# Sums of squares for the main stream's norms: one matmul group per tile of squares in place of adding the tiles up first

## The chip, the cores and the metric

The kernel runs on one core of a Trainium2 chip. The metric is the time of one execution on the device in microseconds (us), the median of several runs. The engines of the core are the tensor engine (PE), the vector engine (DVE), the scalar engine (ACT), GpSimd (POOL) and SyncE (SP), which issues the transfers. Each has its own instruction stream, and they wait for each other through semaphores. [...]

## The reference

The model is two stacks of two layers at 512 tokens and width 1024. The first two layers are hybrids of attention, retention and gated linear attention; the other two have attention and a feed-forward part, and take a second stream of 256 context tokens along. All is float32. What the change touches are the norms of the main stream:

```python
def rms_norm(x, gain=None):
    xf = x.astype(jnp.float32)
    y = xf * lax.rsqrt(jnp.mean(xf * xf, axis=-1, keepdims=True) + EPS)
    ...

def second_block(...):
    ...
        h = rms_norm_2(x, norm_g[l, 0]) * (1.0 + sc1) + sh1
        ...
        x = x + g1 * rms_norm_2(y, norm_g[l, 1])
        h = rms_norm_2(x, norm_g[l, 2]) * (1.0 + sc2) + sh2
        x = x + g2 * rms_norm_2(swiglu(h, ffn_w_in[l], ffn_w_out[l]), norm_g[l, 3])
```

For each token the squares of its 1024 features are summed; the token's features are then scaled by the root's reciprocal, a gain and a shift.

## The kernel before, in words

Activations lie with the features on the 128 partitions and the tokens along the free dimension: `x` is eight tiles of 128 features by 512 tokens (`KD` = 8, `S` = 512; the context has `CL` = 256 tokens). A norm therefore needs a sum over partitions. It is made in these steps. `square` makes a tile's squares on ACT (line 503). `square_sums` adds the eight square tiles up on DVE: six adds at line 515 into the first two, one at line 518. `rstd_cols` then lets PE sum over the partitions: for each of four blocks of 128 tokens the 128x128 block of squares is the stationary operand and a column of ones (`blk`) the moving one, so that each matmul gives one column of 128 sums (the records `<-blk,bp 128x1` at line 389; a float32 matmul runs as two passes, so that four matmuls are eight records). DVE scales the sums (line 481), POOL takes the power -1/2 (line 483), and `spread` brings the result back to all partitions with four transposes (line 498, `<-ident,sm`). `norm_tile` then makes the pairs `hh`, `hl` of high and low parts (lines 554 to 560), from which the dense matmuls work: each product is three matmuls with high and low parts of weights and activations (`wh`, `wl`, made by ACT at line 422 and by POOL or DVE at lines 398 and 400 from the loaded `wr`).

Five times in the program `boundary` joins two layers' halves. It loads x, adds the normed output of the half before (`postnorm_tile`, lines 576 and 577; the adds into x are made by POOL and DVE in turns), stores x, makes the squares and sums, and norms x for the half behind. The square tiles come from the tag `bp`, which has five buffers, in the fifth boundary eight. Boundaries 1 to 4 (at about 464, 961, 1545 and 2030 us of the profile) are woven with work of the context stream, whose dense matmuls show as `<-hc,wh`, `<-hc,wl` and `<-hid,wh`; a function `weave` takes steps of the two streams by fixed rates, and a scheduler, which goes by planned times of the instructions, fixes the order on every engine. Boundary 5 (at 2444 us) is alone; behind it the first matmuls of the feed-forward part (`outer`) start on weights already held (`u0h` and so on).

Of the kernel before, what the change touches and what calls it, by code (L numbers as in the profile page):

```python
# [23 lines left out]
KD = D // 128  # L24
S = 512
# [174 lines left out]
class Net:  # L200
# [266 lines left out]
    def rstd_cols(self, sq_tiles, T, groups, width, add=False, al=None):  # L467

        nc = self.nc
        nt = T // 128  # L470
        groups, add = (self.ones_col, True) if groups is None else (groups, add)
        per = groups.shape[-1]
        n = per if add else per * len(sq_tiles)
        ps = (al or self.std)[1]([128, nt, n])
        m = len(sq_tiles)
        for i, sq in enumerate(sq_tiles):
            for t in range(nt):
                o = ps[:, t, :] if add else ps[:, t, i * per:(i + 1) * per]
                self.mm(o, sq[:, t * 128:t * 128 + 128], groups, i + t == 0, (i, t) == (m - 1, nt - 1))
        ms = self.sm([128, nt, n])  # L480
        nc.vector.tensor_scalar(ms, ps, 1.0 / width, EPS, op0=ALU.mult, op1=ALU.add)  # L481
        r = self.sm([128, nt, n])
        nc.gpsimd.tensor_tensor(r, ms, self.mhalf[:, None, :].to_broadcast([128, nt, n]), op=ALU.pow)  # L483
        return r
# [55 lines left out]
    def prenorm_steps(self, x, T, gain, shift, pool=None, al=None):  # L540

        nc = self.nc
        n = x.shape[1]
        r = self.rstd(self.square_sums([x[:, k, :] for k in range(n)], T, al), T, al=al)
        h = self.new_h(T, pool)
        for k in range(n):
            self.norm_tile(h, x, k, T, r, gain, shift, al)
            yield
        return h
# [1419 lines left out]
```

## Time and profile before

| | |
|---|---|
| median of 3 runs | 2850.54 us (2847.57 to 2851.17) |
| the profiled execution | 2850.94 us, span 2849.2 us |
| PE busy | 87% of the span |
| DVE, ACT, POOL busy | 44%, 42%, 38% |
| mean granted clock of PE | 0.913 |

The profile shows one execution. A busy share is a mean over all stages; which engine ends a wait in one stage is read from the timeline there, where the figure in brackets is the idle time before an instruction and what ended it.

### The profile page before, as it was taken

What the parts mean: (1) busy time and instruction counts of PE and PEld (TensorE: products, weight loads), DVE (VectorE), ACT (ScalarE), POOL (GpSimd) and SP (SyncE); (2) the same over time, 40 slices, a digit from 0 to 9 for tenths busy, and PEclk for the clock granted to TensorE, in tenths of its full rate; (3) what the DMA queues carried; (4) which work ended last, traced back from release to release, by engine and by line L of the source; (5) the groups of instructions that cost most, each with busy time, mean ns of one, the idle gap of its engine ahead of it and who ended that gap; (6) DMA issues with size and microseconds to landing.
All of it is one profiled execution on the core that took longest, in us unless ns stands there. A gap on an engine that the chain in (4) does not pass through costs nothing. (4 is left out here: it accounts for less than half of the span.)

```text
span 2849.2 us, 35397 instructions
## 1 busy us (share of the span) xinstructions
PE 2467.3 (87%) x13052; PEld 2004.1 (70%) x13052; DVE 1262.4 (44%) x2065; ACT 1187.1 (42%) x2227; POOL 1079.5 (38%) x754
## 2 busy tenths in 40 slices
PE   6978897778888886869999999999878969799997
PEld 4755676665666665648998877777766757688886
DVE  3655356245646643445443621212635757421212
ACT  3534364333547534445554422223434636333222
POOL 2435235344533541214355632323542222443334
PEclk9988897888989987879999999999988989899998
DMA  7354553344344652335554444453443254333332
GB/s 241 125 199 166 181 174 136 117 135 165 107 122 142 220 179 90 116 113 157 162 167 141 163 155 170 145 173 115 165 145 105 68 154 121 110 116 97 96 97 74
DMA packets 170817, 400.58 MB, mean 141 GB/s; under 512 B 19378, under 2 KB 60820, under 8 KB 167316
## 3 DMA queue, kind: packets, MB, share of 16 engines
q1 hardware_dynamic: 170644, 398.31, 42.9%
q8 instruction: 104, 1.70, 0.2%
q14 instruction: 69, 0.57, 0.1%
HBM read 339.85 MB, written 58.39 MB: 140 GB/s over the span
## 5 line engine op out<-in xcount | busy, mean ns | idle before, releaser
L398 POOL TENSOR_TENSOR wl<-wr,wh 128x1024 fp32r<-128x1024 f32 (+3 forms) x245 | 537.7, 2196 | 893.6 <-ACT wh L422 449.0
L422 ACT CAST wh<-wr 128x1024 fp32r<-128x1024 f32 (+3 forms) x367 | 353.8, 964 | 731.0 <-PE d L389 282.6
L389 PE MATMUL d<-hh,wh 128*128 128x512 f32 x960 | 399.1, 416 | 19.3 <-ACT hh L556 7.8
L389 PE MATMUL d<-hl,wh 128*128 128x512 f32 x960 | 394.9, 411 | 3.2 <-POOL hl L398 1.2
L389 PE MATMUL d<-hh,wl 128*128 128x512 f32 x960 | 262.0, 401 | 0.0
L400 DVE SCALAR_TENSOR_TENSOR wl<-wr,wh 128x1024 fp32r<-128x1024 f32 (+3 forms) x122 | 151.9, 1245 | 228.8 <-PE d L389 97.9
L389 PEld LDWEIGHTS d<-hh,wh 128*128 128x128 f32 x960 | 190.5, 198 | 62.3 <-ACT hh L556 8.4
L389 PEld LDWEIGHTS d<-hl,wh 128*128 128x128 f32 x960 | 190.3, 198 | 43.2 <-issue 2.5
L389 PEld LDWEIGHTS d<-hh,wl 128*128 128x128 f32 x960 | 183.8, 193 | 39.2 <-issue 1.5
L400 DVE SCALAR_TENSOR_TENSOR pg<-b,pg 128x512 fp32r<-128x512 f32 (+1 forms) x208 | 137.1, 665 | 69.6 <-ACT pg L404 68.2
L934 POOL TENSOR_TENSOR oy<-pg,pg 64x256 f32<-64x256 f32 (+1 forms) x72 | 57.8, 802 | 284.4 <-ACT pg L931 89.4
L389 PE MATMUL b<-hh,wh 128*128 128x512 f32 x416 | 164.5, 395 | 0.0
L389 PE MATMUL b<-hl,wh 128*128 128x512 f32 x416 | 163.5, 393 | 0.0
L404 ACT CAST pg<-b 128x512 fp32r<-128x512 f32 (+1 forms) x208 | 117.3, 571 | 90.9 <-PE b L909 85.4
L882 DVE TENSOR_REDUCE sm<-s 128x1 f32<-128x768 f32 (+3 forms) x144 | 120.8, 846 | 63.8 <-PE s L389 63.4
L389 PE MATMUL d<-hc,wh 128*128 128x256 f32 x656 | 107.4, 315 | 24.2 <-ACT wh L422 11.7
L950 DVE SCALAR_TENSOR_TENSOR rp<-rp,d 128x512 f32<-128x512 f32 (+1 forms) x77 | 46.7, 607 | 166.1 <-ACT rp L949 166.0
L389 PEld LDWEIGHTS d<-hc,wh 128*128 128x128 f32 x656 | 97.0, 216 | 28.8 <-ACT wh L422 12.9
L389 PE MATMUL d<-hid,wh 128*128 128x512 f32 (+1 forms) x528 | 115.5, 363 | 1.6 <-POOL hid L398 1.5
L1738 DVE SCALAR_TENSOR_TENSOR rp<-rp,b 128x512 f32<-128x512 f32 (+1 forms) x64 | 38.1, 596 | 175.5 <-PE b L389 175.0
L389 PE MATMUL b<-hid,wh 128*128 128x512 f32 (+1 forms) x528 | 110.9, 361 | 0.0
L389 PE MATMUL b<-hh,wl 128*128 128x512 f32 x416 | 104.0, 390 | 0.0
(412 smaller groups left out, 5165.5 us busy)
## 6 DMA issues: line engine op xcount, KB each, us to landing
wr<-in_ffn_w_in SPq DMA_DIRECT2D x132, 512.0 KB
mr<-in_ada_w SPq DMA_DIRECT2D x96, 512.0 KB
wr<-in_ffn_w_out SPq DMA_DIRECT2D x48, 512.0 KB
x<-x SPq DMA_DIRECT2D x20, 1024.0 KB
wr<-in_w_in SPq DMA_DIRECT2D x38, 512.0 KB
mr<-in_w_mod SPq DMA_DIRECT2D x32, 512.0 KB
wr<-in_ev_w_in SPq DMA_DIRECT2D x20, 512.0 KB
wr<-in_ffn_w_out SPq DMA_DIRECT2D x24, 384.0 KB
```

Source lines behind the costliest of these rows:

```text
L389: self.nc.tensor.matmul(out, lhsT, rhs, start=start, stop=stop)
L398: self.nc.gpsimd.tensor_sub(out, src, hi)
L400: self.nc.vector.scalar_tensor_tensor(out, src, scale, hi, op0=ALU.mult, op1=ALU.subtract)
L404: self.nc.scalar.copy(hi, src)
L422: nc.scalar.copy(hi[:, :n], raw[:, :n])
L882: nc.vector.reduce_max(c, s, axis=AX.X, negate=True)
L934: nc.gpsimd.tensor_tensor(d, sel(t), sel(rs), op=ALU.mult)
L950: nc.vector.scalar_tensor_tensor(t, t, 1.0, ps, op0=ALU.add, op1=ALU.mult)
L1738: nc.vector.scalar_tensor_tensor(g, g, 0.5, pu, op0=ALU.mult, op1=ALU.mult)
```

## The change

In `prenorm_steps`, for the main stream alone (512 tokens), the squares are no longer added up on DVE. A generator hands the eight square tiles to `rstd_cols` one by one, which makes four matmuls from each and lets PE accumulate all 32 in one PSUM tile. The tile in PSUM is now taken before the first square is made, and the buffer of a square comes free when PE has read it. The context's norms and the start keep the adds.

```diff
--- before.py
+++ after.py
@@ -470,9 +470,9 @@
         nt = T // 128
         groups, add = (self.ones_col, True) if groups is None else (groups, add)
         per = groups.shape[-1]
-        n = per if add else per * len(sq_tiles)
+        m = len(sq_tiles) if isinstance(sq_tiles, list) else KD
+        n = per if add else per * m
         ps = (al or self.std)[1]([128, nt, n])
-        m = len(sq_tiles)
         for i, sq in enumerate(sq_tiles):
             for t in range(nt):
                 o = ps[:, t, :] if add else ps[:, t, i * per:(i + 1) * per]
@@ -541,7 +541,8 @@
 
         nc = self.nc
         n = x.shape[1]
-        r = self.rstd(self.square_sums([x[:, k, :] for k in range(n)], T, al), T, al=al)
+        xs = [x[:, k, :] for k in range(n)]
+        r = self.rstd(self.square_sums(xs, T, al) if T < S else (self.square(t, T, al) for t in xs), T, al=al)
         h = self.new_h(T, pool)
         for k in range(n):
             self.norm_tile(h, x, k, T, r, gain, shift, al)
```

The scheduler orders the instructions anew. The names in the rows that follow are the program's tiles with running numbers, which differ between the two programs; `x4` is four matmuls in succession. First, PE in boundary 5. Before (`b_21041` takes the sums of squares, `b_21050` the transposes):

```order
L389 MATMUL b_20974<-blk,rp_20962 128x1 x4
L498 MATMUL b_20987<-ident,sm_20985 128x128 x4
L389 MATMUL b_21041<-blk,bp_21018 128x1 x4
L498 MATMUL b_21050<-ident,sm_21048 128x128 x4
L389 MATMUL d_21093<-hh_21055,u0h_20782 128x512
```

After (`b_21102` takes the sums, from eight tiles `bp`):

```order
L498 MATMUL b_21071<-ident,sm_21069 128x128 x4
L389 MATMUL b_21102<-blk,bp_21103 128x1 x4
L389 MATMUL b_21102<-blk,bp_21109 128x1 x4
L389 MATMUL b_21102<-blk,bp_21115 128x1 x4
L389 MATMUL b_21102<-blk,bp_21121 128x1 x4
L389 MATMUL b_21102<-blk,bp_21127 128x1 x4
L389 MATMUL b_21102<-blk,bp_21133 128x1 x4
L389 MATMUL b_21102<-blk,bp_21139 128x1 x4
L389 MATMUL b_21102<-blk,bp_21145 128x1 x4
L498 MATMUL b_21155<-ident,sm_21153 128x128 x4
L389 MATMUL d_21198<-hh_21160,u0h_20866 128x512
```

The four matmuls on the added-up tile have become eight groups of four, contiguous, ahead of the same transposes. In boundaries 2 and 4 the eight groups stand contiguous too. In boundary 2 two products of the modulation (`<-mr,mc`) and its selections (`<-mod_sel`), which stood behind the transposes, now stand between the groups and the transposes. In boundary 4 ten matmuls `d<-hc` stood ahead of the group and five behind it; now all sixteen stand behind the transposes. In boundary 3 two groups are contiguous and the others are single matmuls between the context's feed-forward matmuls.

Second, PE in boundary 1, where `d_4015` and `d_4066` are pieces of the context's dense work. Before:

```order
L389 MATMUL d_4015<-hc_3692,wh_4011 128x256 x16
L389 MATMUL d_4015<-hc_3692,wl_4012 128x256 x8
L389 MATMUL d_4066<-hc_3692,wh_4062 128x256 x5
L389 MATMUL s_4157<-blk,bp_4134 128x1 x4
L389 MATMUL d_4066<-hc_3692,wh_4062 128x256 x5
L498 MATMUL s_4166<-ident,sm_4164 128x128 x4
L389 MATMUL d_4066<-hc_3692,wh_4062 128x256 x6
```

After (`s_4134` takes the sums of squares):

```order
L389 MATMUL s_4134<-blk,bp_4135 128x1 x4
L389 MATMUL s_4134<-blk,bp_4141 128x1 x4
L389 MATMUL d_4015<-hc_3692,wh_4011 128x256 x2
L389 MATMUL s_4134<-blk,bp_4147 128x1 x4
L389 MATMUL d_4015<-hc_3692,wh_4011 128x256 x3
L389 MATMUL s_4134<-blk,bp_4153 128x1 x4
L389 MATMUL d_4015<-hc_3692,wh_4011 128x256 x2
L389 MATMUL s_4134<-blk,bp_4159 128x1 x4
L389 MATMUL d_4015<-hc_3692,wh_4011 128x256 x2
L389 MATMUL s_4134<-blk,bp_4165 128x1 x4
L389 MATMUL d_4015<-hc_3692,wh_4011 128x256 x2
L389 MATMUL s_4134<-blk,bp_4171 128x1 x4
```

The first piece, `d_4015`, stood whole ahead of the one group; now two groups stand ahead of it, and the other six within it. The transposes have moved from the second piece into the end of the first.

Third, ACT in the same place, with the norm's first instructions (`hh`, `bp`) and the weight casts `wh`. Before:

```order
L406 ACTIVATE rp_4007<-d_4015 128x256
L556 ACTIVATE hh_4171<-bp_4173,m_110 128x512
L406 ACTIVATE rp_4058<-d_4066 128x256
L560 ACTIVATE bp_4177<-bp_4177,m_110 128x512
L556 ACTIVATE hh_4171<-bp_4182,m_110 128x512
L404 CAST hh_4171<-bp_4177 128x512
L422 CAST wh_4097<-wr_4095 128x1024
L560 ACTIVATE bp_4230<-bp_4230,m_110 128x512
L422 CAST wh_4188<-wr_4186 128x1024
```

After:

```order
L406 ACTIVATE rp_4007<-d_4015 128x256
L557 ACTIVATE hh_4192<-bp_4194,m_110 128x512
L561 ACTIVATE bp_4198<-bp_4198,m_110 128x512
L404 CAST hh_4192<-bp_4198 128x512
L557 ACTIVATE hh_4192<-bp_4203,m_110 128x512
L561 ACTIVATE bp_4251<-bp_4251,m_110 128x512
L404 CAST hh_4192<-bp_4251 128x512
L557 ACTIVATE hh_4192<-bp_4256,m_110 128x512
L422 CAST wh_4097<-wr_4095 128x1024
```

The cast `wh_4097`, for the dense piece behind `d_4066`, had four instructions of the norm ahead of it and now has seven.

## Rows read from the trace of the kernel before

**Rows 1.** The page's first part: busy us, share, instructions of the tensor engine.
```profile
PE 2467.3 (87%) x13052; PEld 2004.1 (70%) x13052; DVE 1262.4 (44%) x2065; ACT 1187.1 (42%) x2227; POOL 1079.5 (38%) x754
```

**Rows 2.** View by tile of `bp`: ns min/median/max, first and last start.
```profile
L389 PE MATMUL s<-blk,bp x32: 164/298/373, 482.7 to 2057.2; 128*128 128x1 f32 x32
...
L515 DVE TENSOR_TENSOR bp<-bp,bp x30: 675/679/2880, 477.6 to 2459.6; 128x512 f32<-128x512 f32 x30
...
L389 PE MATMUL b<-blk,bp x8: 341/352/352, 2461.2 to 2462.6; 128*128 128x1 f32 x8
...
L518 DVE TENSOR_TENSOR bp<-bp,bp x5: 675/1095/2842, 481.6 to 2460.3; 128x512 f32<-128x512 f32 x5
```

**Rows 3.** Timeline of PE, boundary 5: start, length, instruction, [idle before <-releaser].
```profile
2444.34 1.95 PE L389 MATMUL b<-blk,rp 128*128 128x1 f32 x16 [0.66 <-POOL rp L631]
...
2461.15 1.83 PE L389 MATMUL b<-blk,bp 128*128 128x1 f32 x8 [12.70 <-DVE bp L518]
...
2464.34 1.12 PE L498 MATMUL b<-ident,sm 128*128 128x128 f32 x4 [1.35 <-POOL sm L483]
...
2467.05 0.79 PE L389 MATMUL d<-hh,u0h 128*128 128x512 f32 x1 [1.59 <-ACT hh L556]
```

**Rows 4.** Timeline of ACT, then of DVE, boundary 5.
```profile
2450.62 0.63 ACT L503 ACTIVATE bp<-x 128x512 f32<-128x512 f32 x1 [5.55 <-POOL x L577]
...
2456.15 1.67 ACT L503 ACTIVATE bp<-x 128x512 f32<-128x512 f32 x3 [0.77 <-POOL x L577]
...
2460.31 0.69 DVE L518 TENSOR_TENSOR bp<-bp,bp 128x512 f32<-128x512 f32 x1
```

**Rows 5.** Windows around boundary 5: PE, PEld, DVE, ACT, POOL busy, granted clock, DMA.
```profile
2444.00:2447.60 3.60, 1.95 (x16) 1.86 (x16) 0.56 (x2) 0.63 (x1) 3.58 (x3) 1.00 0.46 155
...
2461.00:2471.00 10.00, 6.90 (x21) 5.64 (x22) 5.53 (x10) 3.97 (x7) 2.95 (x3) 0.50 0.00 0
...
2476.00:2490.00 14.00, 14.00 (x62) 11.22 (x61) 0.00 (x0) 0.00 (x0) 0.41 (x1) 1.00 0.00 1
```

**Rows 6.** Timeline of PE, then of ACT, boundary 2.
```profile
986.69 1.87 PE L389 MATMUL s<-blk,bp 128*128 128x1 f32 x8 [6.08 <-DVE bp L518]
...
995.14 3.78 PE L389 MATMUL b<-hc,wh 128*128 128x256 f32 x16 [1.31 <-ACT wh L422]
...
981.74 2.19 ACT L503 ACTIVATE bp<-x 128x512 f32<-128x512 f32 x4 [4.02 <-POOL x L577]
...
984.09 0.63 ACT L503 ACTIVATE bp<-x 128x512 f32<-128x512 f32 x1
```

**Rows 7.** Timeline of PE, then of ACT, boundary 4.
```profile
2055.73 1.84 PE L389 MATMUL s<-blk,bp 128*128 128x1 f32 x8 [1.64 <-DVE bp L518]
...
2065.10 3.32 PE L389 MATMUL d<-hc,wh 128*128 128x256 f32 x16 [3.15 <-ACT wh L422]
...
2048.82 2.44 ACT L503 ACTIVATE bp<-x 128x512 f32<-128x512 f32 x4 [0.42 <-DVE x L577]
```

**Rows 8.** Timeline of PE, boundary 3 (the first row is dense work before it).
```profile
1562.02 2.05 PE L389 MATMUL b<-hc,wh 128*128 128x256 f32 x16
...
1587.09 0.28 PE L389 MATMUL s<-blk,bp 128*128 128x1 f32 x2
...
1606.92 0.97 PE L389 MATMUL b<-hid,wl 128*128 128x256 f32 x6 [2.26 <-POOL wl L398]
```

**Rows 9.** Window of boundary 3, columns as in group 5.
```profile
1575.00:1612.00 37.00, 32.35 (x238) 31.14 (x238) 23.57 (x32) 21.30 (x35) 27.78 (x19) 0.91 0.41 124
```

**Rows 10.** Timeline of PE, then of ACT, boundary 1.
```profile
477.06 3.78 PE L389 MATMUL d<-hc,wh 128*128 128x256 f32 x16 [5.87 <-DVE rp L400]
...
482.74 0.95 PE L389 MATMUL s<-blk,bp 128*128 128x1 f32 x8
...
494.51 3.78 PE L389 MATMUL d<-hc,wh 128*128 128x256 f32 x16 [6.25 <-ACT wh L422]
...
475.50 1.18 ACT L503 ACTIVATE bp<-x 128x512 f32<-128x512 f32 x2 [1.67 <-POOL x L577]
```

## The prediction

> **What bounds the kernel now.** I read the page's first part first: the tensor engine (PE) is busy 87% of the span, twice as much as any other engine [rows 1]. Nothing that takes work from the vector engine (DVE) alone shortens the kernel, then, unless PE was waiting for just that work. So I went on to the view by tile of `bp`, the tile in which the squares lie [rows 2]: 35 adds of 128x512 (30 of line 515, five of line 518), 0.68 us each undisturbed and up to 2.88 us, and 32 + 8 matmul records, eight for each of five boundaries (four fp32 matmuls, each run as two passes). Then I read the timeline at the five places where those eight passes stand. The reader should ask of each place: was PE idle for the last add, and what is PE's price for eight passes? Boundary 5, at 2443 to 2472 us, is the only one with nothing woven into it, and PE waits 12.70 us there for the last add [rows 3]. In boundary 2 the wait is 6.08 us [rows 6], in boundary 4 1.64 us [rows 7]; in boundaries 1 and 3 the eight passes started without a wait, because dense matmuls of the woven stream ran in front of them [rows 8, 10].
>
> **What the change removes and adds.** It removes seven DVE adds per boundary, 35 in all. It adds seven groups of eight passes per boundary, 56 passes each, 280 in all. ACT makes the same eight squares, and POOL's work stays the same. What the adds gave: behind the last square they are a chain that PE sees only where it was waiting. What the groups cost depends on the clock, and the rows have both prices: 0.95 us for eight passes in boundary 1 (0.119 us a pass) [rows 10], and 1.83 to 1.87 us in boundaries 2, 4 and 5 [rows 3, 6, 7], where the granted clock is at its lower level. [...]
>
> Which price? The windows around boundary 5 show it [rows 5]: granted clock 1.00 while sixteen one-column passes ran and then little, 0.50 in 2461 to 2471 although PE is busy 6.90 of those 10 us with the group, the transposes and the first 512-column matmuls, and 1.00 again behind a few us of 512-column matmuls back to back. In no stretch of this trace did the clock rise while only one-column passes ran. I therefore price groups that stand alone at the lower level once the clock has fallen, and keep the upper level as a bound.
>
> [...]
>
> **Boundary by boundary.**
>
> Boundary 5. The first square is there at 2450.62 + 0.63 = 2451.25, the last at 2456.15 + 1.67 = 2457.8; the adds end at 2461.0 [rows 4]. Before, the group ends at 2461.15 + 1.83 = 2462.98. After, PE works from 2451.25 without a break: 8 x 1.83 = 14.6, to 2465.9. What follows (sums scaled, power, transposes, norm, first dense matmul) was at the lower clock before too, and moves by the same: **+2.9**. At the upper price the groups keep pace with the squares and end one group after the last, about 2459: -4, and about 2 more if the dense matmuls behind them are spared their slow start, -6.
>
> Boundary 2. The squares come late because four of them wait for POOL's add into x [rows 6]: three are there early, the others by 984.09 + 0.63 = 984.7. PE's dense work ends at about 980.6 (6.08 before 986.69). Three groups at 0.95 bring it to 983.5; then the clock has fallen, as it does there before, and five at 1.87 end at 992.8, where the one group ended at 988.56. In the new order two of the modulation's products and its selections stand between the groups and the transposes, where they fill the wait for the power; transposes and dense matmuls of the context follow at about 996.9 against 995.14. The norm starts 5.8 later, but the first matmul that needs it has 24 dense ones ahead: **+2**, between -3 (upper price: the last group ends near 985.7 instead of 988.56) and +6 (the norm's delay in full).
>
> Boundary 4. The first four squares are there before PE is free at 2050.3 (2052.64 less the wait of 2.34), the last at 2048.82 + 2.44 = 2051.3 [rows 7]. Eight groups in a row: I take five at 0.95 and three at 1.84, 10.3, to 2060.6; the transposes end about 2.5 later, at 2063.1; 24 dense matmuls of the context, which before stood around the group, now stand behind (3.3 + 1.5, to about 2068). Before, the next such 24 started at 2065.10 after a wait of 3.15, which covers a part: **+3**, between 0 and +6.
>
> Boundary 3. PE is nearly full (32.35 of 37 us) [rows 9] and the clock high: the eight passes are strewn singly between matmuls of the context's feed-forward [rows 8]. 56 passes x 0.119 = 6.7. PE's own waits there (2.26 for a low half on POOL, a few of 0.3, 1.50 for the power) can take some of it: **+5.5**, between +3 and +9 (if some run at the lower clock). DVE loses seven adds in a stretch in which it is busy too; that may bring low halves earlier, which is the +3.
>
> Boundary 1. The clock fell during the stall before 477.06: the next 16 dense matmuls took 3.78 instead of 2.05 [rows 8, 10]. They and the 8 behind them ran ahead of the group, while the squares and adds were made. In the new order two groups stand in front of these 16, and the other six between them. The second square is there at about 476.1: seven groups x 1.85 = 13.0 and 15 dense at 0.236 = 3.5 end at 492.6, against 482.74 + 0.95 = 483.69. Eleven more of this dense piece, the transposes and the next 24 dense follow, to about 500. Before, the piece after that started at 494.51, having waited 6.25 for a weight cast behind a load, and so a good part of the delay is covered; but in the new order of ACT this cast stands behind seven of the norm's instructions instead of four, and the norm starts later. **+6**, between 0 (upper price) and +8.
>
> **Sum.** 6 + 2 + 5.5 + 3 + 2.9 = 19.4. Behind the boundaries are further waits of PE (for loads and round trips through memory), which can take up part of what the first four lose; I take 5 off, about a quarter, as a choice: +14.4. The profiled execution took 2850.94 us (its span is 2849.2), 0.4 above the median of the three runs: 2850.9 + 14.4 = **2865 us**. All lower bounds with the groups at the upper price give the first rival; all upper bounds (8 + 6 + 9 + 6 + 3) give 32, which will hardly come together; I end the range at 2877.
>
> **Rivals.**
> 1. The clock stays up or comes up under the groups. Then: boundary 1 about 0, boundary 2 -3, boundary 3 +5, boundary 4 +1, boundary 5 -5, together -2: about 2849, and 2843 if boundary 3's waits take its share too. For it: PE is busy without a break, which it was not before. Against it: the 0.50 of rows 5 with PE 69% busy. This is the case on the other side; it turns on whether boundary 5's eight groups take 7.6 us or 14.6. Chance 0.16 (faster by over 0.2% in 0.09 of it).
> 2. The groups are slow, but waits further on take up nearly everything except boundaries 3 and 5: 2.9 + 2 to 3 = about +5, 2856. For it: boundary 1's 6.25 and boundary 4's 3.15 for weights. Against it: the casts whose lateness makes these waits move back with the norm. Chance 0.16.
> 3. The squares themselves are held up: with five buffers the sixth square waits for PE's first group, and ACT's casts stand behind it, so that the woven stream starves as well. In boundary 3 the squares stand between weight casts; if three casts there each came a group late, this would be some 3 x 2 us, with boundaries 1 and 4 the same: +30, 2880. Against it: in the new order three squares of boundary 3 stand behind later casts. Chance 0.08.
> The forecast itself has 0.60.
>
> **Chances and range.** 0.2% is 5.7 us, about what a measurement of this kernel can tell from no change. Slower by more: the forecast (0.60), rival 3 (0.08) and a part of rival 2 (0.05): 0.73. Within: rest of rival 2 (0.11) and of rival 1 (0.07): 0.18. Faster: 0.09. The range reaches from rival 1 at 2849 to 2877; the forecast's own is 2857 to 2876.
>
> **What would show it.** In the new trace: boundary 5's eight groups start at about 2451 plus the shift so far and take 14 to 15 us at a granted clock of 0.50 (7 to 8 us would show rival 1); DVE has 35 adds fewer and PE 280 records more; in boundary 3 the stretch from the first group to the first `d<-hh` is longer by some 6 us; in boundary 1 the 16 dense matmuls no longer stand ahead of the groups, and the first `d<-hh` comes some 6 us later. The prediction is wrong if the clock rises under the groups, or if the first four boundaries' delays are gone by the next stage.

## The result, and the profile after

The changed kernel takes 2874.64 us in the median of four runs (2866.98 to 2876.6), the kernel before 2849.06 in four runs beside it: the ratio is 1.0088, with an interval of 1.0067 to 1.0109, or +25 us. In a second, independent set of runs it was 1.0079 (1.0058 to 1.0101), or +22.5 us. The change makes the kernel slower, and by more than the forecast of +14.4; the time lies in the range of 2849 to 2877, near its upper end.

The profiled execution has a span of 2874.8 us. The page's first part, against [rows 1]:

```profile
PE 2514.4 (87%) x13332; PEld 2053.4 (71%) x13332; DVE 1237.7 (43%) x2030; ACT 1187.9 (41%) x2227; POOL 1081.9 (38%) x754
```

PE has 280 records more, as counted, and is 47.1 us longer busy (2514.4 - 2467.3); DVE has 35 instructions less and is busy for 24.7 us less. The work went from an engine at 44% to one at 87%. In the view by tile of `bp`, against [rows 2], the adds are gone, and the matmuls have become 256 + 64:

```profile
L389 PE MATMUL s<-blk,bp x256: 164/352/370, 466.1 to 2076.4; 128*128 128x1 f32 x128
...
L389 PE MATMUL b<-blk,bp x64: 352/352/370, 2474.3 to 2487.8; 128*128 128x1 f32 x64
```

The median of a record is 352 ns in both rows; in `s<-blk` it was 298 before, where a part ran at the upper clock (the eight passes of boundary 1 took 0.95 us [rows 10], with a granted clock of 1.00 in the window 482.70:483.70). Next the timeline of PE in boundary 5, against [rows 3]:

```profile
2474.35 13.81 PE L389 MATMUL b<-blk,bp 128*128 128x1 f32 x64 [2.85 <-ACT bp L503]
...
2492.28 0.80 PE L389 MATMUL d<-hh,u0h 128*128 128x512 f32 x1 [1.66 <-ACT hh L557]
2492.88 0.63 PE L389 MATMUL d<-hh,u1h 128*128 128x512 f32 x1
2493.30 0.63 PE L389 MATMUL s<-hh,u2h 128*128 128x512 f32 x1
```

The 64 passes run without a break for 13.81 us from the moment the first square is there; the wait of 12.70 us has become one of 2.85. The squares come as fast as before (timeline of ACT, against [rows 4]), and the last is done at 2479.21 + 1.67 = 2480.9:

```profile
2473.66 0.63 ACT L503 ACTIVATE bp<-x 128x512 f32<-128x512 f32 x1 [5.68 <-POOL x L578]
...
2479.21 1.67 ACT L503 ACTIVATE bp<-x 128x512 f32<-128x512 f32 x3 [0.77 <-POOL x L578]
```

So at the end of the squares PE still has 7.3 us of passes ahead (to 2474.35 + 13.81 = 2488.2). From the start of the first square to the first dense matmul it is 2492.28 - 2473.66 = 18.6 us; before, 2467.05 - 2450.62 = 16.4 [rows 3, 4]. The windows, with the granted clock, a share of full speed, in the third column from the end, against [rows 5]; the last one is of the kernel before:

```profile
2474.00:2488.00 14.00, 13.65 (x64) 13.66 (x64) 5.69 (x9) 4.26 (x8) 4.65 (x3) 0.50 0.37 150
...
2494.00:2500.00 6.00, 6.00 (x19) 4.68 (x19) 5.76 (x8) 5.28 (x9) 3.53 (x3) 0.66 0.00 0
2500.00:2514.00 14.00, 14.00 (x62) 11.28 (x61) 0.19 (x1) 0.23 (x1) 1.31 (x1) 1.00 0.00 1
...
2471.00:2476.00 5.00, 5.00 (x21) 3.98 (x20) 3.85 (x5) 3.95 (x6) 2.85 (x3) 0.91 0.00 0
```

In the 14 us of the passes PE is busy for 13.65 and its clock is at 0.50; during the first dense matmuls the mean is 0.66, and then 1.00. As an estimate, from a single step between 0.50 and 1.00, the means of 0.66 and, before, 0.91 put the rise at about 2498.1 and 2471.9, which is 5.8 us behind the first dense matmul against 4.8 before. The row of the 14 us decides against the first rival: PE was busy without a break from 2474.35 on, and the clock did not rise.

The other boundaries. Boundary 2, PE, against [rows 6]:

```profile
988.46 9.71 PE L389 MATMUL s<-blk,bp 128*128 128x1 f32 x64
998.10 1.93 PE L389 MATMUL b<-mr,mc 128*32 128x256 f32 x16
...
1000.84 1.09 PE L498 MATMUL s<-ident,sm 128*128 128x128 f32 x4
```

Boundary 4, PE, against [rows 7]:

```profile
2065.41 11.30 PE L389 MATMUL s<-blk,bp 128*128 128x1 f32 x64
...
2078.83 3.39 PE L389 MATMUL d<-hc,wh 128*128 128x256 f32 x16
...
2085.78 2.16 PE L389 MATMUL d<-hc,wh 128*128 128x256 f32 x16 [2.62 <-ACT wh L422]
```

In both, the 64 passes begin when PE would have idled, and take 9.7 and 11.3 us instead of 1.9. In boundary 4 the wait for the cast `wh`, which I had counted as cover, is still there (2.62 of 3.15 us), since the cast stands on ACT behind five of the norm's instructions (2080.00 to 2084.80) and came later with them. Boundary 3, PE, against [rows 8]; the second and third row are two of the single matmuls:

```profile
1591.92 1.84 PE L389 MATMUL s<-blk,bp 128*128 128x1 f32 x16
...
1596.20 0.28 PE L389 MATMUL s<-blk,bp 128*128 128x1 f32 x2
...
1604.72 0.42 PE L389 MATMUL s<-blk,bp 128*128 128x1 f32 x2
...
1607.13 0.90 PE L498 MATMUL s<-ident,sm 128*128 128x128 f32 x3
...
1620.66 1.53 PE L389 MATMUL b<-hid,wl 128*128 128x256 f32 x6 [2.25 <-POOL wl L398]
...
1626.07 0.40 PE L389 MATMUL d<-hh,wh 128*128 128x512 f32 x1
```

The same two places in the kernel before, the transposes and the first dense matmul on the normed x:

```profile
1590.46 0.32 PE L498 MATMUL s<-ident,sm 128*128 128x128 f32 x1 [1.50 <-POOL sm L483]
...
1612.35 0.39 PE L389 MATMUL d<-hh,wh 128*128 128x512 f32 x1
```

From the first group to the first `d<-hh` it is 1626.07 - 1591.92 = 34.15 us; before, 1612.35 - 1587.09 = 25.26 [rows 8]: 8.9 more, where the prediction has some 6. In the new timeline two passes take 0.28 us at 1596.20 and 0.42 at 1604.72. The windows up to 1597 us and behind it:

```profile
1591.90:1597.00 5.10, 5.10 (x47) 5.10 (x46) 0.42 (x1) 2.31 (x5) 2.50 (x2) 0.99 0.51 154
1597.00:1609.90 12.90, 12.83 (x60) 12.53 (x60) 1.99 (x4) 2.18 (x4) 2.83 (x2) 0.50 0.11 30
```

The clock fell at about 1597 us, amid one-column passes in alternation with 256-column matmuls, and for 12.9 us the dense matmuls between them ran at the lower clock (0.50) too. The wait of 2.26 for a low half is still there at 1620.66 (2.25); the 1.50 ahead of the transposes is gone (1607.13). Boundary 1, PE, against [rows 10]:

```profile
466.08 1.05 PE L389 MATMUL s<-blk,bp 128*128 128x1 f32 x8 [2.71 <-ACT bp L503]
468.38 1.86 PE L389 MATMUL s<-blk,bp 128*128 128x1 f32 x8 [1.25 <-ACT bp L503]
470.11 0.77 PE L389 MATMUL d<-hc,wh 128*128 128x256 f32 x2
470.68 1.70 PE L389 MATMUL s<-blk,bp 128*128 128x1 f32 x8
...
481.99 1.70 PE L389 MATMUL s<-blk,bp 128*128 128x1 f32 x8
...
494.55 3.62 PE L389 MATMUL d<-hc,wh 128*128 128x256 f32 x16 [4.28 <-ACT wh L422]
```

Here the two groups ahead of the dense work and the six within it are seen, seven of them at 1.70 to 1.86 us. The dense piece behind them starts at 494.55, after a wait of 4.28: of the 6.25 before, 2 us have covered something, and the rest has moved along. What ends this wait is seen on ACT and in the transfer queue (SP). Before, then after:

```profile
485.65 1.71 SPq L417 DMA_DIRECT2D wr<-in_ev_w_in  x2
493.41 1.04 ACT L422 CAST wh<-wr 128x1024 fp32r<-128x1024 f32 x1 [3.01 <-DMA wr<-in_ev_w_in]
...
473.40 14.77 SPq L817 DMA_DIRECT2D eqc<-rp  x3
488.21 0.95 SPq L417 DMA_DIRECT2D wr<-in_ev_w_in  x2
493.44 1.04 ACT L422 CAST wh<-wr 128x1024 fp32r<-128x1024 f32 x1 [0.59 <-DMA wr<-in_ev_w_in]
```

In both traces the cast waits last for the load of its weights. SP issues that load behind the stores `eqc`, and of these one waits 10.3 us after the change (view of SP's waits: DVE `rp` of line 400) for the products of the dense piece that the groups now hold up. Counted from in front of the boundary, where the changed kernel's execution is 7.7 us ahead, the load is issued some 10 us later. Without the load's last 0.59 us the norm's instructions, which run up to 492.85, would have held the cast: two chains that end almost together, both behind the groups.

The two profiled executions are not in step outside of these places. ACT runs 2227 instructions in each kernel. If the n-th of one execution is set against the n-th of the other, the changed kernel is 7.7 us ahead just in front of boundary 1, where both programs are still the same, and 0.5 ahead behind it (at 520 us); then it is late, by +4.9 at 950, +6.1 at 1530, +13.7 at 1640, +13.5 at 2000, +22.0 at 2190, +22.9 at 2430 and +25.7 at 2490. The +5.4 between 520 and 950 belongs to no boundary. Which of the other steps are the boundaries' costs is not told by one pair of traces.

### The profile page after: what moved, and what is told of

Same layout as the page of the kernel before. It is cut to its first block, busy times and chain, and to the rows that moved or that the text cites. A ratio compares the mean times of both kernels' runs of the same rounds, so it can differ in the third digit from the quotient of the medians.

```text
span 2874.8 us, 35911 instructions
## 1 busy us (share of the span) xinstructions
PE 2514.4 (87%) x13332; PEld 2053.4 (71%) x13332; DVE 1237.7 (43%) x2030; ACT 1187.9 (41%) x2227; POOL 1081.9 (38%) x754
## 5 line engine op out<-in xcount | busy, mean ns | idle before, releaser
L483 POOL TENSOR_TENSOR sm<-sm,mhalf 128x4 f32<-128x4 f32 (+3 forms) x33 | 44.8, 1358 | 157.5 <-DVE sm L481 147.7
```

## Experiments

**One boundary at a time.** `prenorm_steps` counts its calls for the main stream and takes the sums without adds in one of the five alone (here the third). The edits of this part are against the changed kernel:

```diff
-        xs = [x[:, k, :] for k in range(n)]
-        r = self.rstd(self.square_sums(xs, T, al) if T < S else (self.square(t, T, al) for t in xs), T, al=al)
+        xs = [x[:, k, :] for k in range(n)]; self.bnd = getattr(self, "bnd", 0) + (T == S)
+        r = self.rstd((self.square(t, T, al) for t in xs) if T == S and self.bnd in (3,) else self.square_sums(xs, T, al), T, al=al)
```

Boundary 1:

> Only boundary 1 takes its sums without the adds; the four others keep them. Theory A (the groups' passes cost PE 0.21 to 0.23 us each at the lower clock, and the delay stays to the end): +5 to +8 us, the whole shift of that place in the changed kernel's trace (from 7.7 ahead to 1.2 ahead). Rival B (the waits for weights behind boundary 1 take the delay up; the 6.5 of the trace were a difference of two executions that was there before): 0 to +2 us.

Measured: ratio 1.0017 (1.0001 to 1.0033), +4.8 us, just below theory A, with rival B's 2 inside the interval; the table below decides for A. Boundary 2:

> Only boundary 2. Theory A: the groups start 4.7 us earlier than the one group did and take 9.7 instead of 1.9, and the dense work behind them comes 2 to 3 us later, in front of which nothing is needed at once: 0 to +3 us. Rival B (the norm's delay of some 5 us goes through in full): +5 to +6 us.

Measured: 0.9993 (0.9978 to 1.0009), -2.0 us: no cost, and not rival B's +5. Boundary 3:

> Only boundary 3. Theory A: +7 us (56 passes x 0.119 = 6.7 and the dense matmuls between them at the lower clock; the changed kernel's trace shows +7.6 there). Rival B (the waits of 2.26 and 1.5 us behind it absorb a part): +3 to +4 us.

Measured: 1.0014 (1.0000 to 1.0029), +4.0 us: both expectations lie in the interval, and the table below decides for A. The window of its passes, with a mean clock of 0.64:

```profile
1588.00:1612.00 24.00, 23.67 (x133) 23.07 (x133) 7.97 (x11) 8.63 (x15) 8.02 (x7) 0.64 0.12 34
```

Boundary 4:

> Only boundary 4. Theory A: 56 more passes are 64 records in 11.3 us, of which the earlier start and the 3.15 us wait hide a half; +4 to +7 us. Rival B (the long wait for the q transfer behind it, 11.3 us, takes it up): 0 to +2 us.

Measured: 1.0019 (1.0003 to 1.0036), +5.4 us, as in theory A. The wait that rival B names (for `gq`) is 12.9 us in this trace against 11.3 before, and so has not taken anything up. In the timeline of PE the passes are as in the full change, and the wait for the cast behind them as well:

```profile
2043.96 11.29 PE L389 MATMUL s<-blk,bp 128*128 128x1 f32 x64
...
2064.34 3.78 PE L389 MATMUL d<-hc,wh 128*128 128x256 f32 x16 [2.63 <-ACT wh L422]
```

Boundary 5:

> Only boundary 5, where nothing is woven in. Theory A: PE runs 64 passes in 13.8 us at a granted clock of 0.50 from the first square on; +2.5 to +3 us, and nothing behind it can absorb that. Rival (the groups' end is set by the squares, not by the passes): -3 to -4 us.

Measured: 1.0010 (0.9997 to 1.0023), +2.8 us, as in theory A; the rival's gain is outside the interval. The window of its passes:

```profile
2446.00:2460.00 14.00, 13.81 (x64) 13.72 (x64) 5.50 (x9) 3.98 (x7) 4.32 (x3) 0.50 0.37 150
```

**The kernel before, once more.**

> The kernel before, unchanged, for a second trace of it: how far two executions of one program drift apart at the boundaries. Between the two traces so far, the stretches ahead of boundary 1 and between boundaries 1 and 2, where both programs are the same, differ by -7.5 and +6 us. If that is drift between executions, it shows here in the same size, and the time is the same within 0.2%.

Measured: 1.0002 (0.9985 to 1.0018). Its single runs lie between 2839.81 and 2855.43 us. Its trace is 7.5 us ahead of the first one at 450 us, without any change, as the changed kernel's was; so that difference is drift between executions. Between 520 and 950 us this trace shows no drift (+0.7), but the change's own second trace (below) has -3.0 there, where the first has +5.4. In boundary 1 the first row of [rows 10] stands 7.7 us earlier:

```profile
469.38 3.78 PE L389 MATMUL d<-hc,wh 128*128 128x256 f32 x16 [5.89 <-DVE rp L400]
```

With these traces each boundary's own cost can be read. The table gives, for each execution, by how much its lag against the first trace of before grew over a boundary, as the difference of two medians (of the start times of ACT's n-th instructions within 12 us of a mark): marks at 450 and 520 us for boundary 1, 950 and 1160 for 2, 1530 and 1640 for 3, 2000 and 2190 for 4, 2430 and 2490 for 5. Bold is where the boundary was changed.

| execution | 1 | 2 | 3 | 4 | 5 |
|---|---|---|---|---|---|
| before, again | +1.3 | +1.0 | +0.2 | -3.5 | 0.0 |
| boundary 1 alone | **+7.6** | +2.3 | 0.0 | -0.4 | +0.2 |
| boundary 2 alone | +1.3 | **+1.0** | -0.2 | -0.6 | 0.0 |
| boundary 3 alone | +1.4 | -0.1 | **+9.2** | -0.2 | +1.0 |
| boundary 4 alone | +0.1 | -0.1 | +0.8 | **+4.5** | +0.3 |
| boundary 5 alone | -2.4 | 0.0 | 0.0 | -3.6 | **+3.0** |
| the change | **+7.2** | **+0.8** | **+7.7** | **+8.5** | **+2.7** |
| the change, again | **+6.5** | **-0.1** | **+7.8** | **+2.6** | **+2.9** |

The mean of the bold ones less the mean of the others in a column is +6.8, -0.1, +8.1, +6.9 and +2.6, together +24. Boundary 4's is the least certain, since its unchanged values differ by 3.4 and its changed ones by 5.9. Most of that spread arises far behind the groups: with marks at 2030 and 2080 the same reckoning gives +4.0, +5.1 and +4.1 where the boundary was changed (alone, the change, the change again) and -1.0 to +0.5 in the five others, so that the boundary itself costs about +4.5, and the five together about +22. The times of the five single kernels add up to +15.0 (4.8 - 2.0 + 4.0 + 5.4 + 2.8); each is uncertain by about 4, so their sum by 9 or more, since four of them share one set of runs of the kernel before.

**The change once more.**

> The change as it is, timed in more rounds. The five boundaries changed one at a time gave +4.8, -2.0, +4.0, +5.4 and +2.8 us, +15 together, each uncertain by some 4; the change as a whole gave +25 in four runs. Theory A (the boundaries' costs add up, and the first figure was high by the drift between executions): +14 to +20 us. Rival B (the places reinforce each other, because the scheduler orders everything anew): +24 us or more.

Measured: 1.0079 (1.0058 to 1.0101), +22.5 us, between the two expectations and within the sum's uncertainty. In the table the bold values of the five single kernels add up to 25.3, those of the change's two traces to 26.9 and 19.7, so no reinforcement shows: I take the costs as adding up. Whether later waits give a few us back, as the +15 of the single kernels' times would have it, the times leave open.

**Filling between the groups (boundary 5).** A 512-column matmul behind each group, to bring the clock up; its result goes to a spare tile and is not used. The identity is the stationary operand and the tile of squares the moving one, the other way round than the expectation says. A second part of the edit, not shown, keeps the change to boundary 5.

```diff
+        fill = None if isinstance(sq_tiles, list) else self.wide()
         for i, sq in enumerate(sq_tiles):
             for t in range(nt):
...
+            if not isinstance(sq_tiles, list):
+                self.mm(fill[:, 0, :], self.ident, sq, True, True)
```

> Only boundary 5, and behind each tile's four matmuls one matmul more with the tile as stationary blocks against the identity, 512 columns into a spare PSUM tile, whose result nobody reads. If the price of the groups is the clock, which 512-column matmuls between them bring up: after the first two or three tiles eight passes take 0.95 instead of 1.72 us, the groups with the filling take no longer than without (14 us or less for twice the work) and the dense matmuls behind start at the upper clock: between -3 and +1 us against the kernel with boundary 5 alone changed. If the clock stays down: 8 x 0.85 us more, +7 us.

Measured: 1.0041 (1.0025 to 1.0056), +11.7 us against the kernel before, 8.9 more than with boundary 5 alone. The timeline of PE and the windows:

```profile
2457.90 2.05 PE L389 MATMUL s<-bp,ident 128*128 128x512 f32 x2
2459.75 1.71 PE L389 MATMUL b<-blk,bp 128*128 128x1 f32 x8
...
2480.23 1.71 PE L389 MATMUL b<-blk,bp 128*128 128x1 f32 x8
...
2486.36 0.79 PE L389 MATMUL d<-hh,u0h 128*128 128x512 f32 x1 [1.66 <-ACT hh L560]
```

```profile
2456.00:2470.00 14.00, 13.83 (x41) 9.70 (x42) 5.51 (x9) 4.08 (x8) 4.47 (x3) 0.50 0.37 150
2470.00:2484.00 14.00, 14.00 (x43) 9.71 (x42) 0.16 (x1) 0.00 (x0) 1.02 (x1) 0.50 0.00 0
...
2490.00:2496.00 6.00, 6.00 (x28) 4.83 (x27) 4.18 (x6) 4.01 (x6) 3.67 (x3) 1.00 0.00 0
```

The expectation of a rising clock was wrong. PE does not idle for 27 us, half of this in 512-column passes, and the clock is 0.50 throughout; it rose only amid the dense matmuls behind, and was at 1.00 from 2490 on. The expectation's price was too low as well: from the start of one group to the next it is 3.41 us ((2480.23 - 2459.75) / 6), of which the group has 1.71, so that the filling takes 1.70 and not 0.85, which is about two dense 512-column matmuls at 0.50 (0.42 us from the start at 2492.88 to the next at 2493.30 after the change).

**The squares as the moving operand.** A column of ones is stationary, the 512 tokens move; eight tiles accumulate into one row, DVE copies it, four small matmuls turn it into columns.

```diff
+        if not isinstance(sq_tiles, list):
+            total = al[1]([128, T])[:1]
+            for i, sq in enumerate(sq_tiles):
+                self.mm(total, self.ones_col, sq, i == 0, i == m - 1)
+            row = al[0]([128, T])[:1]
+            nc.vector.tensor_copy(row, total)
+            sq_tiles, groups, m = [row], self.ones_row[:, :1], 1
```

> All five boundaries, but the squares are the moving operand: a column of ones stationary, 512 tokens moving, so that eight tiles are 16 passes of 512 columns into one row of sums; DVE copies the row, and four small matmuls turn it into columns. No adds on DVE either. Theory A (what costs is the number of weight loads and one-column passes at a low clock): about 0.43 us a pass at the lower clock and 0.23 at the upper, so PE keeps pace with the squares in boundary 5 (-1 to -2 us there), +3 to +4 us in boundary 3, +7 us in all. Rival (any sum on PE holds up the woven stream in the same way, whatever its passes): +15 to +25 us.

Measured: 1.0036 (1.0016 to 1.0055), +10.3 us: less than half of the change's cost. It is nearer to the +7 of theory A, but the interval (+4.6 to +15.7) just holds the rival's 15 too. Boundary 5, timeline of PE and windows:

```profile
2460.76 9.98 PE L389 MATMUL b<-bp,blk 128*1 128x512 f32 x16 [2.85 <-ACT bp L510]
2471.51 1.05 PE L389 MATMUL b<-ones_row,bp 1*128 1x1 f32 x8 [0.77 <-DVE bp L481]
```

```profile
2460.70:2464.00 3.30, 3.24 (x4) 0.31 (x5) 3.30 (x6) 1.46 (x4) 2.77 (x3) 0.50 0.19 79
2464.00:2468.00 4.00, 4.00 (x7) 0.67 (x6) 2.10 (x3) 2.51 (x5) 1.58 (x1) 0.66 0.75 309
2468.00:2472.00 4.00, 3.23 (x12) 0.91 (x10) 0.68 (x1) 0.00 (x0) 0.00 (x0) 1.00 0.37 150
```

Here the clock did rise, from 0.50 to 1.00, during sixteen 512-column passes with nothing else between them. The price of a pass was too low in the expectation: 9.98 / 16 = 0.62 us as a mean of both levels, where 0.43 was expected for the lower one and 0.23 for the upper, which is about what a dense 512-column matmul takes (0.42 as above; 14.00 / 62 = 0.23 at 1.00 [rows 5]). They still end early enough that boundary 5 costs nothing (+0.3 by the table's reckoning); boundaries 2 and 3 cost +8.7 and +6.1, and 1 and 4 lie within the unchanged ones' spread. So theory A's total came about with other places than it named. In boundary 2 the new order sets the modulation's products between the passes, and PE waits there for their load:

```profile
983.26 1.94 PE L389 MATMUL b<-mr,mc 128*32 128x256 f32 x16 [4.42 <-DMA mr<-in_ada_w]
```

At least a part of the +8.7 is thus the order's, and this kernel does not isolate the price of the passes.

**How many tiles to leave.** `square_sums` is told how many tiles it shall leave; four adds and four tiles, or six adds and two tiles:

```diff
-        r = self.rstd(self.square_sums(xs, T, al) if T < S else (self.square(t, T, al) for t in xs), T, al=al)
+        r = self.rstd(self.square_sums(xs, T, al, *(("nnnnvvvv", 4) if T == S else ())), T, al=al)
...
```

> Half of the change in all five boundaries: DVE makes four adds into four tiles, and PE takes four groups instead of one or eight. Theory A (the price is that of the added groups, three in place of seven): three sevenths of the whole, +6 to +9 us. Rival B (a sum on DVE that is cut short pays by itself up to some point): 0 or less.

Measured: 1.0020 (1.0003 to 1.0037), +5.7 us: just under theory A's range, with rival B's 0 outside the interval.

> Only the last add is left out: six adds into two tiles, and PE takes two groups. One add of 0.68 us undisturbed (up to 2.84) against one group more, 0.95 us at the upper clock and 1.85 at the lower. Theory A: one seventh of the whole, +1 to +3 us. Rival B (the last add is at the end of the chain, and its slow execution beside POOL is what is saved, and the first group runs under the adds): -1 to -3 us.

In the trace of the kernel before the slow executions do stand beside POOL: the last add took 0.68 and 0.69 us in boundaries 1 and 5, where POOL had no instruction running, and 1.09, 2.84 and 2.59 in boundaries 2, 3 and 4, beside instructions of POOL of 0.92, 2.40 and 2.37 us. Measured: 0.9987 (0.9970 to 1.0004), -3.7 us. Since that is on the other side of theory A's +1 to +3, it was run again:

> The kernel with two tiles once more, since it came out between -8.5 and +1.1 us against the kernel before and is the only one that may beat it. If its gain is real (the trace puts it into boundary 1, -4.9 us, and boundary 3, -1.6): -2 to -5 us again. If it was drift: within 2 us of the kernel before, and boundary 1 within the -2.4 to +1.4 us by which unchanged boundaries 1 differ.

Measured: 0.9986 (0.9967 to 1.0004), -4.0 us. Twice the same size, and each time the interval just includes no change. Of the two places that the expectation named, boundary 1 does not hold: it changed by -4.9 us in the first trace and by -0.5 in the second, which is within the unchanged ones' spread. Boundary 3 does, with -1.6 and -1.5 where the unchanged ones have -0.2 to +0.8. Where the rest of a gain of 4 us would come from stays open. Of all kernels here it is the fastest in the median, and clearly faster than the change; that it beats the kernel before is likely, not shown.

## Why the prediction was right, and which of its terms were off

The direction and the mechanism hold; the size was too low, +14.4 where +25 and +22.5 were measured, and the range was wide enough for it. **What bounds the kernel**: PE does; 24.7 us less of DVE bought nothing that is seen in the time, and 47 us more of PE busy time go with a cost of 22 to 25.

**The price of a pass** was the right one: the groups that stand alone in boundary 5 ran at the lower clock (0.50), at 0.22 us a pass (13.81 / 64; 11.30 / 64 = 0.18 in boundary 4, where the first ones were still fast: the clock was 1.00 in the window 2065:2068 and 0.50 in 2068:2072). I had taken 0.23, from a group of eight that stood behind an idle stretch. What a pass consists of is not separated: its weight loads are busy as long as the passes are (PEld 13.66 of the 14 us in boundary 5), and no run has one-column passes without a load for each.

**Boundary 5** (+2.9): by the traces +2.6 over the unchanged ones. The passes were shorter than 14.6 by 0.8, the first dense matmul came 2.2 us later, and the rest is that the clock rose 1.0 us later behind it. At the upper price the prediction has a gain of 4 to 6 us for this boundary; the sum of the forecast does not use it.

**Boundary 1** (+6): +6.8. The groups' price and place are as described, and of the wait for the cast 2 us became cover and 4.28 stayed. The reason given for that, seven of the norm's instructions in front of the cast, is only one half: the load of the weights, late behind the stores on SP, ended the wait in the new trace as in the old one.

**Boundary 2** (+2): -0.1. Here the groups' early start does pay for their length: they took 9.7 us where I had 3 x 0.95 + 5 x 1.87 = 12.2.

**Boundary 3** (+5.5): +8.1. The size was off: I priced 56 passes at the upper clock and took a part off for PE's waits. Of the waits that I named the 1.50 did go and the 2.25 stayed, but the clock was down for 12.9 us amid the passes, for the dense matmuls between them too (0.50, against a mean of 0.84 between 1586.6 and 1597 us before). The bound of +9 "if some run at the lower clock" was the better figure.

**Boundary 4** (+3): +6.9 by the table, with the widest spread, and about +4.5 by the closer marks. What was off is the cover: the wait of 3.15 us for `wh` took up only 0.5 us of the delay, because it moved along with the norm's instructions in front of the cast.

**The 5 us taken off the sum** for later waits are the third term, by its size the largest, and the one that had no row behind it. None of the five single kernels' traces shows such a return beyond the drift that the kernel before shows against itself. Without it the sum was 19.4, and with boundaries 3 and 4 as measured it is 19.4 - 5.5 - 3 + 8.1 + 4.5 = 23.5. That it is wrong is likely, not shown: the traces' +22 less 5 is 17, inside the second interval of the change (+16.5 to +28.8) and below the first (+19 to +31).

**The rivals.** The first (the clock comes up under the groups, 2849) is refuted by 0.50 in the windows of the change and of boundary 5 alone, and by the clock's fall amid the passes of boundary 3. The second (waits take up the rest, 2856) is refuted at the waits it named: 4.28 of 6.25 and 2.62 of 3.15 us are still there behind the delay. The third (squares held up) exists, but is small. Boundary 5, with its eight buffers, cannot show it; in the four others ACT does wait for PE before a square, six times, 0.26 to 0.90 us each (view by source of line 503 after the change; before it, the view has no such line):

```profile
PE s L389: 3.5, 6
```

That is 3.5 us on an engine that is busy 41% of the span, against the +30 of this rival. How much of boundary 3's +8.1 it makes, where two of the six stand (0.85 and 0.73), is not shown.

## What to carry to other kernels

Work that is moved from a half-idle engine to the one that bounds the kernel has to be paid there wherever that engine has no idle time for it (boundary 2 had, with a wait of 6.08 us before, and cost -0.1; boundary 3, with PE busy for 32.35 of 37 us, cost 8.1), and the saving on the other engine counts only where the bounding engine was waiting for it. Price the added work at the clock that it will find, and ask what it does to the clock of its neighbours: the one-column matmuls strewn between dense ones cost boundary 3 8.1 us, not the 6.7 that they had been priced at by the upper clock, with the clock at 0.50 for 12.9 us. A wait behind the changed place is no cover if what ends it hangs on the same chain (4.28 of 6.25 and 2.62 of 3.15 us stayed); look at what stands ahead of the awaited instruction on its own engine, and ahead of its load in the transfer queue.

## What the runs showed of the hardware that was not expected

A stretch of 27 us in which PE never idled, alternately with eight one-column and two 512-column passes, ran at a granted clock of 0.50 from end to end, while during sixteen 512-column passes alone, with one stationary column, it rose to 1.00 (0.50, 0.66 and 1.00 in three windows in succession). A float32 pass with 512 columns took 0.85 us at the lower clock (1.70 for the two of the filling), twice the 0.42 of a 512-column matmul of the dense kind (from the start at 2492.88 to the next at 2493.30 in boundary 5, also at 0.50), which is one record where the float32 one is two. And two executions of the same program drifted apart by 7.5 us within the first 450 us, so that a single pair of traces says nothing on differences of that size unless it is read place by place.
